# Reciprocal roots of a hybrid diffusion block: VectorE's Newton rounds or GpSimd's power

## The chip, the cores and the metric

The kernel runs on one core of a Trainium2 chip. The metric is the device time of one execution in microseconds. A core has five engines that run side by side, each with its own queue in a fixed order: TensorE (PE, matmuls and transposes), VectorE (DVE), ScalarE (ACT), GpSimd (POOL) and SyncE (SP, which only issues DMAs here). PE's weight loads are listed as PEld.

## The reference

Two layers of a diffusion backbone on 512 latent tokens and 256 context tokens of width 1024, in float32. Each layer is a mixer of four parallel branches (grouped-query attention with rotary positions, Mamba-2 SSD in both directions, S5, a gated short convolution), merged by gates and projected, then an expert-choice mixture of 16 SwiGLU experts. The context tokens leave after the first layer's experts. A reciprocal root of a mean of squares stands in five places:

```python
def rmsnorm(x, g):
    y = xf * lax.rsqrt(jnp.mean(xf * xf, axis=-1, keepdims=True) + RMS_EPS)
    return (y * g.astype(F32)).astype(x.dtype)
h_l = modulate(rmsnorm(x, norm_mix_g[i]), mod_l[0], mod_l[1])           # before the mixer
ql = axial_rope(rmsnorm(heads(q_l, ATTN_HEADS), q_norm_g), ...)         # q and k heads, width 64
return rmsnorm(y * jax.nn.silu(z), norm_g)                              # SSD, width 512
expert_choice_ffn(modulate(rmsnorm(x, norm_ffn_g[i]), ...), ...)        # before the router
return rmsnorm(x, final_norm_g)                                         # at the end
```

## The kernel before, in words

Tokens stand in tiles of 128 on the partitions: tiles 0 and 1 are context, 2 to 5 latent. `run` calls, for each layer, `mixer` (norm, branches, merge) and `moe`. Weights are streamed from HBM by SyncE; dense products split each operand into a high and a low part and take three matmuls (L99 to L101, the splits are L114 on ScalarE and L115 on VectorE).

`rsqrt` (L118) computes out = (x*scale + eps)^-0.5 for n numbers per partition. L124 forms v, L125 and L126 make a first guess by a shift and a subtraction on the bits, and three Newton rounds follow: L134 to L136 in the long form, three instructions a round, or L130 and L131 in the short one, two a round after a scaling of v in L128. All of it is on VectorE, 12 instructions long or 10 short. It is called 30 times:

- `norm` (L337), once a layer, n=6: the root of all six tiles, then the scaling of each tile (L339), then transposes (L344) and modulation (L347 to L349). It is marked high priority.
- `finish` in `ssd` (L846), once per tile (6 and 4), n=1: squares summed by ScalarE (L844), the root, y times root and gain (L847), transposes (L850). GpSimd does S L819 (half of the heads), y L835 (first layer) and segr L800 here.
- `attention` (L919), three times a layer, n=12 for keys and n=24 for two halves of the queries: sums of squares (L907), the root, R times root (L922), copies on GpSimd (L928), transposes (L929).
- `merge` (L574), once per tile (6 and 4), n=1, the short form: the root scales the router's logits (L580) and the rows that the experts gather (L594). Output projections (L99 to L101) of the next tile run beside it. After the last latent tile `places` (L1514 to L1518) takes the top tokens per expert on VectorE, and `gather` makes indices (L1536) and fetches rows with indirect DMAs from GpSimd's queue (L1538). Weight loads from a certain one on wait until the first gather has started (`wafter`).
- `last` in `moe` (L1681), twice at the very end, n=2: the final norm of two tiles each (L1680 sums, L1684 to L1686 scale, L1687 stores).

While a branch works through its chain, matmuls of gates, short convolution and modulation weights ("filling", psmm tiles) are laid into TensorE's queue beside it. The order in each engine's queue is not the program's: a list scheduler fixes it when the program is built, by priority and by its own model of how long each instruction takes. Semaphores for the dependences are added after that.

Of the kernel before, what the change touches and what calls it, by code (L numbers as in the profile page):

```python
# [9 lines left out]
F32 = mybir.dt.float32  # L10
# [3 lines left out]
I32 = mybir.dt.int32  # L14
AF = mybir.ActivationFunctionType
OP = mybir.AluOpType
# [42 lines left out]
class Kern:  # L59
# [58 lines left out]
    def rsqrt(self, pool, out, x, scale, eps, n, short=False):  # L118

        nc = self.nc  # L120
        v = pool.tile([128, n], F32, name="rs_v", tag=f"rsv{n}")
        y = pool.tile([128, n], F32, name="rs_y", tag=f"rsy{n}")
        t = pool.tile([128, n], F32, name="rs_t", tag=f"rst{n}")
        nc.vector.tensor_scalar(v, x, scale, eps, op0=OP.mult, op1=OP.add)  # L124
        nc.vector.tensor_scalar(t.bitcast(I32), v.bitcast(I32), 1, None, op0=OP.logical_shift_right)  # L125
        nc.vector.tensor_scalar(y.bitcast(I32), t.bitcast(I32), -1.0, float(0x5F3759DF), op0=OP.mult, op1=OP.add)  # L126
        if short:
            nc.vector.tensor_scalar(v, v, -0.5, None, op0=OP.mult)  # L128
            for i in range(3):
                nc.vector.tensor_scalar(t, y, y, v, op0=OP.mult, op1=OP.mult)  # L130
                nc.vector.tensor_scalar(out if i == 2 else y, t, 1.5, y, op0=OP.add, op1=OP.mult)  # L131
            return
        for i in range(3):
            nc.vector.tensor_mul(t, y, y)  # L134
            nc.vector.scalar_tensor_tensor(t, t, -0.5, v, op0=OP.mult, op1=OP.mult)
            nc.vector.scalar_tensor_tensor(out if i == 2 else y, t, 1.5, y, op0=OP.add, op1=OP.mult)  # L136

    def constants(self, pool, first, last):

# [6 lines left out]
    def setup(self):  # L146
        nc, tc, I = self.nc, self.tc, self.I
        self.cp = cp = self.ctx.enter_context(tc.tile_pool(name="cp", bufs=1))
        self.vt = "a"
        self.filling = True  # L150
        cT = cp.tile([128, 8, 2], F32, name="cT")
        nc.sync.dma_start(cT, I["cT"])
        self.cst = {}
        self.constants(cp, "ident", "one")
        self.ident = self.cst["ident"]
        self.identb = cp.tile([128, 128], BF16, name="identb")
        nc.vector.tensor_copy(self.identb, self.ident)
        th = cp.tile([128, 8, 2], F32, name="cth")
        nc.scalar.activation(th, cT, AF.Tanh, scale=0.5)
        self.cpad = cp.tile([128, 8, 32], F32, name="cpad")  # L160
        nc.vector.memset(self.cpad, 0.0)
        nc.vector.tensor_scalar(th, th, 1.0, 0.5, op0=OP.add, op1=OP.mult)
        nc.vector.tensor_mul(self.cpad[:, :, 0:2], th, cT)
        self.gm = cp.tile([128, 2, 2, 8], F32, name="gm")
        nc.scalar.dma_start(self.gm, I["gm"])
        self.bmT = cp.tile([128, 2, 48], F32, name="bmT")
        nc.scalar.dma_start(self.bmT, I["bmT"])
        self.modT, self.amod = {}, {}
        self.affT = cp.tile([16, 768], F32, name="affT")
        dr = lambda nm, *s: tc.dram_tile(list(s), F32, name=nm)  # L170

        self.xs = dr("xs", 512, D)
        self.xc = dr("xc", 256, D)
        self.mrow = {(l, q): dr(f"mrow{l}{q}", 2, D) for l in range(2) for q in (2, 5)}
        self.zs = dr("zs", 768, 512)
        self.ys = [dr(f"ys{b}", 128, 4, 768) for b in range(4)]
        self.gs = [dr(f"gs{b}", 8, 128, 768) for b in range(4)]

        self.s5w = dr("s5w", 6, 128, self.S5W)
        self.s5r = dr("s5r", 128, 24)  # L180

        self.hr = [[dr(f"hr{l}{s}", n, D) for s, n in enumerate((512, 256)[:2 - l])] for l in range(2)]
        self.afd = [[dr(f"afd{l}{s}", n, 16) for s, n in enumerate((512, 256)[:2 - l])] for l in range(2)]
# [1709 lines left out]
```

## Time and profile before

| what | value |
|---|---|
| median of 3 runs | 3041.78 us (3039.12 to 3045.5) |
| the profiled execution, its own time | 3042.23 us |
| its span, first to last instruction | 3040.5 us |
| mean granted TensorE clock | 0.971 of full speed |
| busy: PE, DVE, ACT, POOL | 2771.3, 1561.6, 786.6, 518.7 us |
| HBM traffic | 222 GB/s over the span |

A line of the timeline gives the start, the length, the engine, the line of the kernel, the operation, the tile written and the tile read with their shapes, and in brackets how long the engine had stood idle before and what released it. Several like instructions in a row are merged (x3). In the waits, a line says who waited for whom, us in total, how often, and the longest.

### The profile page before, as it was taken

The page shows a single profiled execution, that of the slowest core. Times are in us where ns is not written, and L with a number is a line of the kernel's source. Part 1 is how long each engine was busy: PE and PEld are TensorE (multiplying, and loading weights), DVE is VectorE, ACT ScalarE, POOL GpSimd, SP SyncE. Part 2 cuts the span into 40 slices and gives each one's busy share as a digit, 9 for nine tenths or more (in the row PEclk, how much of TensorE's full clock was granted, in tenths as well). Part 3 has the DMA queues.
Part 4 walks back from the last instruction along what each step waited for, and adds up shares of the span by engine and source line. Part 5 has one row for each costly group of instructions (what it writes and reads, how often), then busy time and mean ns, then how long its engine had stood idle before and what let it go on. Part 6 is the DMA issues. An engine that isn't in the chain of part 4 may idle for free. (4 is left out here: it accounts for less than half of the span.)

```text
span 3040.5 us, 47083 instructions
## 1 busy us (share of the span) xinstructions
PE 2771.3 (91%) x18626; PEld 1817.4 (60%) x18626; DVE 1561.6 (51%) x3583; ACT 786.6 (26%) x1749; POOL 518.7 (17%) x693
## 2 busy tenths in 40 slices
PE   7999978999999979899999989999999996998887
PEld 4866756787878964344333358577877883332223
DVE  5468588555516664544431354768564454322223
ACT  4354223325622310001110133323364221000001
POOL 1022075120004122111111010400200221100001
PEclk9999989999999989999999989999999997999999
DMA  7324523411146559899999843264214577999997
GB/s 240 108 72 124 164 86 113 132 38 59 56 155 218 184 191 384 337 392 345 361 374 399 337 150 106 61 213 166 80 50 158 168 272 291 409 409 409 409 409 299
DMA packets 332542, 678.69 MB, mean 223 GB/s; under 512 B 22945, under 2 KB 198305, under 8 KB 331554
## 3 DMA queue, kind: packets, MB, share of 16 engines
q1 hardware_dynamic: 297712, 610.31, 55.5%
q10 hardware_dynamic: 27666, 43.19, 3.9%
q0 software_dynamic: 6944, 22.19, 2.4%
q8 instruction: 147, 2.41, 0.3%
q14 instruction: 73, 0.60, 0.1%
HBM read 613.09 MB, written 60.94 MB: 222 GB/s over the span
## 5 line engine op out<-in xcount | busy, mean ns | idle before, releaser
L1578 PE MATMUL psa<-we,X 128*64 128x512 f32 (+1 forms) x4096 | 583.9, 491 | 37.0 <-DMA we<-in_w_exp_gate_dram 18.7
L1578 PEld LDWEIGHTS psa<-we,X 128*64 128x64 f32 (+1 forms) x4096 | 203.5, 123 | 391.6 <-issue 273.1
L99 PE MATMUL psmm<-hH,fwH 128*128 128x512 f32 x984 | 371.4, 377 | 7.7 <-DVE xpad L640 3.8
L101 PE MATMUL psmm<-hH,fwL 128*128 128x512 f32 x984 | 365.9, 372 | 2.2 <-DVE fwL L115 2.2
L100 PE MATMUL psmm<-hL,fwH 128*128 128x512 f32 x984 | 365.8, 372 | 0.0
L1610 PE MATMUL psa<-we,hidT 128*64 128x512 f32 x992 | 234.4, 610 | 18.6 <-ACT hidT L1598 13.0
L99 PEld LDWEIGHTS psmm<-hH,fwH 128*128 128x128 f32 x984 | 189.5, 193 | 50.3 <-issue 12.9
L101 PEld LDWEIGHTS psmm<-hH,fwL 128*128 128x128 f32 x984 | 189.4, 192 | 31.8 <-issue 5.2
L100 PEld LDWEIGHTS psmm<-hL,fwH 128*128 128x128 f32 x984 | 189.9, 193 | 30.8 <-issue 8.4
L1591 ACT ACTIVATE hid<-psa 128x512 f32<-128x512 f32 (+1 forms) x48 | 25.2, 526 | 547.7 <-PE psa L1578 481.3
L1610 PEld LDWEIGHTS psa<-we,hidT 128*64 128x64 f32 x992 | 68.7, 139 | 159.9 <-issue 115.7
L115 DVE TENSOR_TENSOR fwL<-fr,fwH 128x1024 fp32r<-128x1024 f32 (+1 forms) x100 | 109.0, 1091 | 101.1 <-ACT fwH L114 91.8
L1592 DVE SCALAR_TENSOR_TENSOR hid<-hid,psa 128x512 f32<-128x512 f32 (+1 forms) x48 | 28.7, 598 | 254.0 <-ACT hid L1591 254.0
L1618 DVE SCALAR_TENSOR_TENSOR y<-psa,ag,m 64x512 f32<-64x512 f32 x62 | 46.5, 750 | 204.6 <-PE psa L1610 204.0
L475 POOL TENSOR_TENSOR merged<-merged,tgm 128x512 f32<-128x512 f32 (+1 forms) x48 | 62.6, 1324 | 479.1 <-DVE tgm L473 478.8
L1565 POOL TENSOR_TENSOR X<-X,modT 128x512 f32<-128x512 f32 x40 | 42.9, 1083 | 521.8 <-DVE X L1564 452.8
L99 PE MATMUL psa<-cwH,hH 128*128 128x256 f32 (+1 forms) x432 | 123.3, 285 | 1.3 <-DVE R L909 1.2
L101 PE MATMUL psa<-cwH,hL 128*128 128x256 f32 (+1 forms) x432 | 122.2, 283 | 0.0
L100 PE MATMUL psa<-cwL,hH 128*128 128x256 f32 (+1 forms) x432 | 122.1, 283 | 0.0
L114 ACT CAST fwH<-fr 128x1024 fp32r<-128x1024 f32 (+1 forms) x100 | 89.5, 896 | 123.4 <-DMA fr<-in_w_in_dram 67.3
L420 ACT ACTIVATE tg<-psmm 128x512 f32<-128x512 f32 x96 | 50.7, 529 | 191.4 <-PE psmm L101 188.0
L1593 DVE TENSOR_TENSOR hid<-hid,psa 128x512 f32<-128x512 f32 (+1 forms) x48 | 28.7, 598 | 135.0 <-PE psa L1578 134.4
(566 smaller groups left out, 5714.4 us busy)
## 6 DMA issues: line engine op xcount, KB each, us to landing
we<-in_w_exp_gate_dram SPq DMA_DIRECT2D x128, 1024.0 KB
we<-in_w_exp_up_dram SPq DMA_DIRECT2D x128, 1024.0 KB
we<-in_w_exp_down_dram SPq DMA_DIRECT2D x128, 1024.0 KB
fr<-in_w_mod_dram SPq DMA_DIRECT2D x96, 512.0 KB
fr<-in_w_in_dram SPq DMA_DIRECT2D x64, 512.0 KB
raw<-in_w_in_dram SPq DMA_DIRECT2D x36, 512.0 KB
gs<-tg ACTq DMA_DIRECT2D x32, 384.0 KB
tgm<-gs SPq DMA_DIRECT2D x32, 384.0 KB
```

What stands on the lines that cost most here:

```text
L99: self.nc.tensor.matmul(ps, ah, bh, start=start and i == 0, stop=False)
L100: self.nc.tensor.matmul(ps, ah, bl, start=False, stop=False)
L101: self.nc.tensor.matmul(ps, al, bh, start=False, stop=stop and i == n - 1)
L114: self.nc.scalar.copy(h, x)
L115: self.nc.vector.tensor_sub(l, x, h.bitcast(F32))
L420: nc.scalar.activation(tg[:, o:o + n], self.cm(w, m, o, n), AF.Tanh, scale=0.5)
L475: (V if i == 3 else nc.gpsimd).tensor_add(dst, dst, t)
L1565: nc.gpsimd.tensor_add(X[:, hk], X[:, hk], Bm[:, 24 + h * 4:28 + h * 4, s:s + 1].to_broadcast([128, 4, 128]))
L1578: self.lastup = nc.tensor.matmul(ps[s][j * c:(j + 1) * c], X[s][:, k, r:r + c], w(k)[:, j * n:(j + 1) * n], start=k == 0, stop=k == 7, ski ...
L1592: V.scalar_tensor_tensor(hid, hid, 1.0, g, op0=OP.add, op1=OP.mult)
L1610: ins = nc.tensor.matmul(ps[j * c:(j + 1) * c], lh, w(k)[:, j * n:(j + 1) * n], start=k == 0, stop=k == 7, skip_group_check=True)
L1618: self.lasty = V.scalar_tensor_tensor(Y[s][r, nn], ps[j * c:(j + 1) * c], got[s][1][r, e:e + 1], m5[s][r, nn], op0=OP.mult, op1=OP.mult)
```

## The change

`rsqrt` becomes two instructions on GpSimd: v = x*scale + eps, and v to the power -0.5, the exponent read from a tile `half` that VectorE fills once at the start. Both forms, long and short, become this one; the tiles for the guess and the rounds go. No call site is edited.

```diff
         v = pool.tile([128, n], F32, name="rs_v", tag=f"rsv{n}")
-        y = pool.tile([128, n], F32, name="rs_y", tag=f"rsy{n}")
-        t = pool.tile([128, n], F32, name="rs_t", tag=f"rst{n}")
-        nc.vector.tensor_scalar(v, x, scale, eps, op0=OP.mult, op1=OP.add)
-        nc.vector.tensor_scalar(t.bitcast(I32), v.bitcast(I32), 1, None, op0=OP.logical_shift_right)
-        nc.vector.tensor_scalar(y.bitcast(I32), t.bitcast(I32), -1.0, float(0x5F3759DF), op0=OP.mult, op1=OP.add)
-        if short:
-            nc.vector.tensor_scalar(v, v, -0.5, None, op0=OP.mult)
-            for i in range(3):
-                nc.vector.tensor_scalar(t, y, y, v, op0=OP.mult, op1=OP.mult)
-                nc.vector.tensor_scalar(out if i == 2 else y, t, 1.5, y, op0=OP.add, op1=OP.mult)
-            return
-        for i in range(3):
-            nc.vector.tensor_mul(t, y, y)
-            nc.vector.scalar_tensor_tensor(t, t, -0.5, v, op0=OP.mult, op1=OP.mult)
-            nc.vector.scalar_tensor_tensor(out if i == 2 else y, t, 1.5, y, op0=OP.add, op1=OP.mult)
+        nc.gpsimd.tensor_scalar(v, x, scale, eps, op0=OP.mult, op1=OP.add)
+        nc.gpsimd.tensor_tensor(out, v, self.half[:, :n] if n == 1 else self.half.to_broadcast([128, n]), op=OP.pow)
...
         self.cp = cp = self.ctx.enter_context(tc.tile_pool(name="cp", bufs=1))
+        self.half = cp.tile([128, 1], F32, name="half")
+        nc.vector.memset(self.half, -0.5)
```

## Rows read from the trace of the kernel before

**Rows 1.** Page, part 1: busy us (share of the span) and instructions.
```profile
PE 2771.3 (91%) x18626; PEld 1817.4 (60%) x18626; DVE 1561.6 (51%) x3583; ACT 786.6 (26%) x1749; POOL 518.7 (17%) x693
```

**Rows 2.** Groups by line, VectorE: busy us, mean ns, idle before.
```profile
L134 DVE TENSOR_TENSOR rs_t<-rs_y 128x1 f32<-128x1 f32 (+4 forms) x60 | 14.9, 249 | 1.4
```

**Rows 3.** Timeline, VectorE: first and last step of three roots, SSD and attention.
```profile
313.28 0.15 DVE L124 TENSOR_SCALAR rs_v<-ssy 128x1 f32<-128x1 f32 x1 [0.84 <-ACT z L844]
...
315.39 0.16 DVE L136 SCALAR_TENSOR_TENSOR rsy<-rs_t,rs_y 128x1 f32<-128x1 f32 x1
255.71 0.15 DVE L124 TENSOR_SCALAR rs_v<-ssy 128x1 f32<-128x1 f32 x1
...
264.05 0.16 DVE L136 SCALAR_TENSOR_TENSOR rsy<-rs_t,rs_y 128x1 f32<-128x1 f32 x1
641.11 0.17 DVE L124 TENSOR_SCALAR rs_v<-ssq 128x24 f32<-128x24 f32 x1
...
646.20 0.18 DVE L136 SCALAR_TENSOR_TENSOR rq<-rs_t,rs_y 128x24 f32<-128x24 f32 x1
```

**Rows 4.** PE's waits: 200 to 330 (two), 600 to 700, 2140 to 2210, 1935 to 1995.
```profile
PE psa L850 <- DVE y L847: 6.7, 5, 2.5
PE psmm L99 <- DVE xpad L640: 1.0, 1, 1.0
PE psa L929 <- POOL kd L928: 3.8, 4, 1.6
PE psa L929 <- POOL kd L928: 2.2, 3, 1.5
PE psmm L99 <- DVE cv L643: 1.1, 1, 1.1
```

**Rows 5.** Groups by line and shape, GpSimd: busy us, mean ns, idle before.
```profile
L819 POOL TENSOR_TENSOR S<-S,E 128x128 f32<-128x128 f32 x40 | 21.8, 546 | 83.4 <-DVE S L818 80.0 <-PE psmm L101 1.2 <-DVE rs_y L126 1.1
L1538 POOL DMA_INDIRECT xg<-hr,xi x20 | 20.0, 1002 | 79.3 <-DVE xi L1536 39.0 <-DVE x L1017 23.3 <-issue 6.4
L603 POOL MEMSET xpad<- 128x1 f32 x72 | 3.9, 124 | 156.8 <-DVE cv L619 100.2 <-PE psb L1610 24.6 <-DVE modT L208 24.5
```

**Rows 6.** Timeline, GpSimd and VectorE: single instructions at 262, 676 and 1941.
```profile
262.31 0.46 POOL L819 TENSOR_TENSOR S<-S,E 128x128 f32<-128x128 f32 x1 [0.42 <-DVE S L818]
...
676.54 0.73 POOL L917 TENSOR_TENSOR R<-R,tp 128x256 f32<-128x256 f32 x1 [2.10 <-DVE rs_v L124]
676.58 0.73 DVE L125 TENSOR_SCALAR rs_t<-rs_v 128x24 int32<-128x24 int32 x1
...
1941.53 1.04 POOL L800 TENSOR_TENSOR segr<-cst,dt 128x512 f32<-128x512 f32 x1 [0.27 <-PE psa L806]
```

**Rows 7.** Timeline, VectorE: the roots of the two layers' first norms.
```profile
14.05 0.17 DVE L124 TENSOR_SCALAR rs_v<-ss 128x6 f32<-128x6 f32 x1 [9.49 <-ACT junk L335]
...
16.27 0.17 DVE L136 SCALAR_TENSOR_TENSOR rstd<-rs_t,rs_y 128x6 f32<-128x6 f32 x1
...
1752.89 0.17 DVE L124 TENSOR_SCALAR rs_v<-ss 128x6 f32<-128x6 f32 x1 [1.23 <-ACT junk L335]
...
1758.15 2.08 DVE L339 TENSOR_SCALAR x<-x,rstd 128x1024 f32<-128x1024 f32 x3
```

**Rows 8.** Timeline, VectorE: last root and indices of layer 0's router; layer 1's last logits.
```profile
1114.86 0.12 DVE L124 TENSOR_SCALAR rs_v<-ss 128x1 f32<-128x1 f32 x1
...
1122.83 0.15 DVE L1536 CAST xi<-fi 128x1 int32<-128x1 f32 x1
...
2529.06 0.23 DVE L580 SCALAR_TENSOR_TENSOR lg<-psa,rstd,cb 128x16 f32<-128x16 f32 x1 [0.29 <-PE psa L578]
```

**Rows 9.** Windows: us, busy (instructions) of PE, PEld, DVE, ACT, POOL; PEclk, DMA, GB/s.
```profile
2705.00:3016.00 311.00, 260.06 (x1168) 86.20 (x1165) 73.54 (x114) 19.48 (x33) 14.67 (x15) 1.00 1.03 406
```

**Rows 10.** Timeline, VectorE: the final norm's first sum, and its last four scalings.
```profile
3028.76 0.15 DVE L1680 TENSOR_TENSOR ss<-ss 128x2 f32<-128x2 f32 x1
...
3034.36 0.48 DVE L1685 SCALAR_TENSOR_TENSOR x<-x,rs,g 128x256 f32<-128x256 f32 x1
...
3035.42 0.35 DVE L1686 TENSOR_SCALAR x<-x,rs 128x256 f32<-128x256 f32 x1
```

## The prediction, made before the changed kernel ran

> **What bounds the kernel now.** I read the page's busy times first: TensorE is busy 91% of the span, VectorE 51%, GpSimd 17% [rows 1]. A change that moves work from VectorE to GpSimd can therefore gain only where TensorE, or the weight stream, stands still because of a reciprocal root. So I looked next at the roots themselves (the groups by line), then at when each of the 30 calls starts and ends (the timeline), and last at what TensorE waits for in those stretches (the waits).
>
> The roots take 340 VectorE instructions: 20 calls of 12 and 10 short ones of 10. The largest group, L134 with 60 of them, takes 14.9 us [rows 2]; with the other groups of L124 to L136 in that view it is about 69 us, 2.3% of the span. Nearly all of it lies beside TensorE work. Undisturbed, a chain of 12 takes 2.3 us (313.28 to 315.55); where the scheduler has laid other VectorE work between its steps it takes 8.5 us (255.71 to 264.21) or 5.3 us (641.11 to 646.38) [rows 3]. That is what TensorE notices: it waited 6.7 us for L847 (the line behind the root) in the first layer's SSD, and 3.8 and 2.2 us for the copies that follow the root in the two attentions [rows 4].
>
> **The change, part by part.** Each call becomes two GpSimd instructions: a multiply-add T, and a power X of n elements per partition. Added in all: 60 GpSimd instructions, and one VectorE memset at the start, before VectorE has anything to do, so at nothing.
>
> *Price of T.* The nearest rows are a 128x1 memset, 0.124 us, and a two-input 128x128 multiply, 0.546 us [rows 5]. I take 0.2, nearer the first, as it reads one tensor of few elements.
>
> *Price of X.* No power runs in the trace. From below, the memset, 0.12 us. From above I charge every element per partition as much as that whole 128x128 multiply, on top of the 1.0 us of GpSimd's slowest small instruction, the indirect DMA (1002 ns): 1.0 + 0.46n, with 0.46 for an undisturbed multiply [rows 5, 6]. That is 1.5 us for n=1 and 12 us for n=24. I take X = 0.65 + 0.06n as an estimate: a fixed part between multiply and indirect DMA, and 40 times the multiply's step per element, since the multiply grows from 0.46 us at 128 elements to 1.04 us at 512, 1.5 ns each [rows 6]. So 0.7 us for n=1 or 2, 1.0 for 6, 1.4 for 12, 2.1 for 24. With three handovers between engines at 0.1 us each (an estimate; a step of an undisturbed chain starts 0.2 us after the one before and takes 0.15) the root of one element is ready 1.2 us after its sum instead of 2.3 or more, and that of 24 after 2.6 instead of 4.1, the mean of the four such calls, of which 641.11 is the longest [rows 3].
>
> Now place by place, in order of time. Each term is what TensorE, or the end, gets back.
>
> - First norm (n=6): the chain runs from 14.05 to 16.44 with VectorE otherwise idle [rows 7]. After: 0.3 + 0.2 + 1.0 = 1.5 us instead of 2.4. Scaling and transposes follow at once: 0.8.
> - SSD, first layer, six calls: waits of 6.7 us for L847 and 1.0 us for L640, which stands in VectorE's queue among the steps of a root [rows 4]. The longest, 2.5 us, follows an undisturbed chain and can shrink by 2.3 - 1.2 = 1.1 us; the other 5.2 us could go altogether, 6.3 at best. What is late next is L847 itself, in order behind chunk work on VectorE. I take half: 3.0.
> - Attention, both layers, six calls (four of 24, two of 12): with roots 1.5 us (n=24) and 2.4 us (n=12) earlier, up to 5 of the 6.0 us of waiting [rows 4] could go; gate matmuls fill TensorE up to that point and hide the rest. Half: 2.5.
> - Router of layer 0: the last context tile's root (1114.86 to 1120.40) is interleaved with the top-k of the latent tokens on a full VectorE, and the gather's indices (1122.83) come behind both [rows 8]. Adding up the spacing of its ten starts gives 1.65 us. The first expert matmul waits for that gather: 1.5. The other nine router roots lie beside output-projection matmuls: 0.
> - Second norm: 1752.89 to 1758.11, 5.2 us, because a weight split (L115, 1.21 us) and small work run between the steps; scaling starts at 1758.15 [rows 7]. After, the root is ready at 1754.4, and scaling can start behind L115 at 1755.25. Of these 2.9 us some goes to matmuls that wait for w_mod: 1.6.
> - SSD, second layer: a wait of 1.1 us for L643 [rows 4] and another of 1.0 for L640, which follow root steps in VectorE's queue: 0.8.
> - Router of layer 1, last tile: the logits (L580) start at 2529.06, released by TensorE, so the root isn't late there [rows 8]; but its steps delay the copies of hT that TensorE needs: 0.8. The weight stream runs at a DMA share of 1.03 from 2705 to 3016 [rows 9], and at 1.02 from 2557 on, so later gains inside that expert stage are worth nothing; this one counts, since the stream restarts behind the gather.
> - Final norm, two calls of n=2: on VectorE they run one behind the other, and the last scaling ends at 3035.77 [rows 10]. After: the first root is ready at 3028.91 + 0.3 + 0.2 + 0.7 = 3030.1, the second at 3031.0. VectorE needs 1.41 us for the four scalings behind a root (3034.36 to 3035.77), so the eight run from 3030.1 to 3032.9: 2.9, of which I take 2.2, since ScalarE's scalings run beside them and may end later.
>
> Sum: 0.8 + 3.0 + 2.5 + 1.5 + 1.6 + 0.8 + 0.8 + 2.2 = 13.2 us. The profiled execution took 3042.2 us (span 3040.5), so 3029.0; the median of the runs is 0.4 us below the profiled one, which I leave aside.
>
> **A rule weighed.** GpSimd and VectorE hold each other up already: a step of the root on 24 elements, whose like took 0.17 us [rows 3], took 0.73 us and ended with the GpSimd addition that had begun 0.04 us earlier [rows 6]. The Trainium skill (SBUF — State Buffer, Who interferes with whom) says that the two share one pair of ports, that whoever issues first holds it for the whole instruction, and that the other is blocked, not throttled. The trace agrees, 0.73 against 0.17 us. By that rule each power could stop VectorE for its whole length, which is rival B.
>
> **Rivals.**
> - A, the slow side: the power is dear per element. Place: the six attention roots, whose R (L922) and kd copies (L928) wait for them. At 0.65 + n*p against today's 4.1 us (n=24, four times) and 4.3 us (n=12, twice), attention loses 120p - 18 us, counted with 0.5 us for T and handovers. That eats the 10.7 us of the other places from p = 0.24 us (6.4 us for n=24) on. At p = 0.46 attention loses 37 us; if gate matmuls cover a third it is 25, the other places keep 10, and the time is 3057. For: nothing in the trace bounds it. Against: GpSimd's rows grow by only 1.5 ns per element [rows 6].
> - B, gain given back: the powers (about 30 us in all, 36 with T) block VectorE, and GpSimd's queue, in order, holds S L819 and y L835 behind a root that waits for its sum. SSD and attention then gain nothing and ten SSD calls cost 0.3 us each: 13.2 - 6.3 + 3 leaves 3.9, 3038.3. For: the 0.73 us above. Against: 69 us of VectorE work goes, twice what comes to GpSimd.
> - C, the scheduler: it fixes every queue's order from its own durations, so 340 instructions fewer and 60 more give another order in all stages. SSD and attention pack roots, chunk work and filler into the same queues, and an order that leaves TensorE 15 us more idle there eats the gain: 3044. This can also help. For: chains of 2.3 us stretched to 8.5 show how freely it interleaves.
> - That the change doesn't do what it says: the root may fail to come off VectorE only if the power were lowered to other instructions, which I give no chance of its own.
>
> **How the numbers follow.** Forecast (a quick power, 3020 to 3036): 0.50. A: 0.22. B: 0.18. C: 0.10. With X at the memset's price all places give at most 22 us: 3020. With X at its upper end 3057 to 3069. I leave out a tenth at either end: 3019 to 3055; the forecast's own range is 3020 to 3036. This kernel's runs tell about 0.2%, 6 us, from no change. Faster than that: the forecast and a little of B and C, 0.52; within: most of B, half of C, a little of A, 0.24; slower: most of A and some of C, 0.24.
>
> **What would show it.** In the changed profile: groups L124 to L136 gone from VectorE and its busy time some 65 us lower; a GpSimd power group whose mean for n=1 is near 0.7 us and for n=24 near 2 us (A: over 6); TensorE's wait for L847 in the first SSD down from 6.7 to about 3 us; scaling in the second norm 2 to 3 us after its sums; the last scaling within 6 us of the last sum of squares. Wrong are: a power over 2 us for one element; TensorE's waits for S L819 or kd L928 grown (B); or a gain or loss in a stage that holds no root (C).

## The result, and the profile after

The changed kernel takes 3070.3 us, median of 4 runs (3069.01 to 3071.5), beside 3043.5 us for the kernel before on the same chip: ratio 1.0089, 95% interval 1.0072 to 1.0105. That is some 27 us slower, where 13 us faster was forecast; it lies above the widest range stated (3019 to 3055) and above the slow end of rival A (3069). In the code after, lines behind `rsqrt` are 11 lower than before; T is L122 and the power L123.

Part 1 of the page, against [rows 1]:

```profile
PE 2776.5 (90%) x18626; PEld 1825.5 (59%) x18626; DVE 1502.9 (49%) x3244; ACT 788.8 (26%) x1749; POOL 565.9 (18%) x753
```

VectorE lost 59 us of busy time and GpSimd gained 47. TensorE executes the same 18626 matmuls; it is 5 us longer busy with them and stands idle 22 us longer (291.7 us of the span instead of 269.2).

The powers themselves, groups by line and shape on GpSimd (busy us, mean ns, idle before):

```profile
L123 POOL TENSOR_TENSOR rq<-rs_v,half 128x24 f32<-128x24 f32 x4 | 16.7, 4170 | 0.3
L123 POOL TENSOR_TENSOR rstd<-rs_v,half 128x1 f32<-128x1 f32 x10 | 5.6, 562 | 0.8
L123 POOL TENSOR_TENSOR rsy<-rs_v,half 128x1 f32<-128x1 f32 x10 | 5.5, 551 | 0.8
L123 POOL TENSOR_TENSOR rq<-rs_v,half 128x12 f32<-128x12 f32 x2 | 4.6, 2290 | 0.2
L123 POOL TENSOR_TENSOR rstd<-rs_v,half 128x6 f32<-128x6 f32 x2 | 2.7, 1346 | 0.2
L123 POOL TENSOR_TENSOR rs<-rs_v,half 128x2 f32<-128x2 f32 x2 | 1.5, 755 | 0.2
```

A line through these is 0.40 us + 0.157 us per element: a quick root for one number (0.56 us), as long as the whole Newton chain for 24 (4.17 us).

TensorE's waits after, in the stretches of [rows 4]: first layer's SSD (200 to 330), the two attentions (590 to 700, 2140 to 2215):

```profile
PE psa L839 <- DVE y L836: 2.8, 2, 1.9
...
PE psa L918 <- POOL kd L917: 9.2, 3, 4.7
...
PE psa L918 <- POOL kd L917: 9.1, 3, 4.5
```

The SSD wait fell from 6.7 to 2.8 us; those in the attentions rose from 3.8 and 2.2 to over 9. One attention call of layer 1, from the timeline of all engines:

```profile
2170.25 0.41 DVE L896 TENSOR_REDUCE ssq<-sq 128x4 f32<-128x256 f32 x1
...
2170.75 0.21 POOL L122 TENSOR_SCALAR rs_v<-ssq 128x24 f32<-128x24 f32 x1 [2.76 <-DVE ssq L896]
...
2171.04 4.17 POOL L123 TENSOR_TENSOR rq<-rs_v,half 128x24 f32<-128x24 f32 x1
...
2173.49 0.40 PE L100 MATMUL psmm<-hL,fwH 128*128 128x512 f32 x1
2175.19 0.72 POOL L906 TENSOR_TENSOR R<-R,tp 128x256 f32<-128x256 f32 x1
2175.94 1.22 DVE L911 TENSOR_TENSOR R<-R,rq 128x1024 f32<-128x1024 f32 x1 [4.40 <-POOL R L906]
2177.30 1.65 POOL L917 COPY kd<-R 128x128 f32<-128x128 f32 x6 [1.39 <-DVE R L911]
2177.64 0.94 PE L918 MATMUL psa<-cst,kd 128*128 128x128 f32 x3 [3.75 <-POOL kd L917]
2178.24 0.78 PE L101 MATMUL psmm<-hH,fwL 128*128 128x512 f32 x1
```

Read it downwards: the power ends at 2175.21; the addition to R (L906), whose result L911 reads, stands behind it in GpSimd's queue and costs another 0.72 us; TensorE's last filling matmul ends at 2173.89, 3.75 us before the transposes can start; and the filling matmul behind that idle time takes 0.78 us instead of 0.40: the granted clock has gone from 2.4 to 1.2 GHz.

The same call in the kernel before:

```profile
2168.50 0.42 DVE L907 TENSOR_REDUCE ssq<-sq 128x4 f32<-128x256 f32 x1
...
2174.78 0.18 DVE L136 SCALAR_TENSOR_TENSOR rq<-rs_t,rs_y 128x24 f32<-128x24 f32 x1
...
2175.93 0.40 PE L100 MATMUL psmm<-hL,fwH 128*128 128x512 f32 x1
...
2176.77 0.80 PE L929 MATMUL psa<-cst,kd 128*128 128x128 f32 x3 [0.43 <-POOL kd L928]
```

From the last sum of squares to the transposes that wait for it, the chain of the four calls with 24 columns takes 7.7 us on average in both kernels. What became shorter is the filling work beside it: past that sum it lasted 5.5 to 7.5 us before, and lasts 3.2 to 3.7 us now. In layer 1 these were 30 and 25 filling matmuls, and now are 13 and 13.

Over whole attention windows the clock shows as PEclk (columns as in [rows 9]). First the changed kernel, 590 to 700 and 2140 to 2215; then the second window before (the first had 730 matmuls, also at 1.00):

```profile
590.00:700.00 110.00, 100.76 (x708) 85.81 (x705) 54.74 (x166) 37.84 (x96) 34.70 (x75) 0.94 0.24 75
2140.00:2215.00 75.00, 64.08 (x388) 55.56 (x388) 36.61 (x107) 20.93 (x40) 32.12 (x62) 0.93 0.17 50
```

```profile
2140.00:2215.00 75.00, 72.85 (x442) 61.96 (x440) 46.20 (x136) 26.27 (x52) 20.28 (x56) 1.00 0.21 64
```

Such a window is cut by the clock on the wall, so its count mixes what was laid there with how fast it ran. Counted from event to event, layer 1 shows what was laid (matmuls on TensorE):

| stretch of layer 1 | before | after |
|---|---|---|
| first transpose of the norm to last transpose of the SSD | 1217 | 1174 |
| from there to the attention's first transpose (L929) | 1034 | 998 |
| the attention, to its last transpose of that line | 321 | 302 |
| from there to the first expert matmul | 1952 | 2060 |

So 108 matmuls more come behind the attention, and only 19 of them left the attention itself; the stretches of SSD and S5 lost more. The last stretch takes 377 us instead of 351, and the first expert matmul of layer 1 comes at 2586.0 instead of 2556.5.

### The profile page after: what moved, and what is told of

It reads as the page before. It is cut to its first block, busy times and chain, and to the rows that moved or that the text cites. A ratio compares the mean times of both kernels' runs of the same rounds, so it can differ in the third digit from the quotient of the medians.

```text
span 3068.2 us, 46800 instructions
## 1 busy us (share of the span) xinstructions
PE 2776.5 (90%) x18626; PEld 1825.5 (59%) x18626; DVE 1502.9 (49%) x3244; ACT 788.8 (26%) x1749; POOL 565.9 (18%) x753
## 5 line engine op out<-in xcount | busy, mean ns | idle before, releaser
L99 PE MATMUL psmm<-hH,fwH 128*128 128x512 f32 x984 | 370.9, 377 | 13.4 <-DVE modT L196 5.2
L99 PEld LDWEIGHTS psmm<-hH,fwH 128*128 128x128 f32 x984 | 189.8, 193 | 54.5 <-issue 11.8
L99 PE MATMUL psa<-cwH,hH 128*128 128x256 f32 (+1 forms) x432 | 122.6, 284 | 0.6 <-DVE dtv L694 0.5
```

What stands on the lines that cost most here:

```text
L99: self.nc.tensor.matmul(ps, ah, bh, start=start and i == 0, stop=False)
```

## The experiments

Theory M: the scheduler counts the power as short and lays less filling work beside the root; on the chip the chain behind it ends later than the filling work, TensorE idles, drops to the low clock and does the rest of the filling later. Theory C: any new order costs this, whatever the roots last. All runs were timed over 5 rounds beside the kernel before; "+n us" below is what the ratio makes of 3043 us. In all variants a root is a power only at the sites named. Where they differ from the changed kernel in the constant -0.5, it stands in a column of an old tile. The edits are shown shortened. Places in an order are compared in the traces, by operation, shapes and tile names without buffer numbers.

**e1: the same order, no long power.**

```diff
-        nc.gpsimd.tensor_tensor(out, v, half, op=OP.pow)
+        nc.gpsimd.tensor_tensor(out, v, half, op=OP.mult if site == "attn" else OP.pow)
```

> The changed kernel, instruction for instruction in the same order on every engine, but in the six attention calls GpSimd multiplies by -0.5 where it took the power (so q and k are scaled wrongly there). Theory M (the long power of 12 and 24 columns starves TensorE, which idles, drops to the low clock and does the filling matmuls late): the instruction falls from 4.17 us to under 0.4 us, TensorE's waits on kd in the two attention windows from 9 us each to under 3 us, the granted clock there comes back to near 1.00, and 15 to 25 us of the 27 are gone: 3045 to 3055 us. Theory C (the new order alone costs the time, whatever the power lasts): the waits elsewhere stay and the time stays at 3064 to 3070 us.

Measured: 3049.9 us, ratio 1.0025 (1.0014 to 1.0035). The groups on GpSimd, the waits in the two attentions, and the window 2140 to 2215 of this run:

```profile
L127 POOL TENSOR_TENSOR rq<-rs_v,half 128x24 f32<-128x24 f32 x4 | 0.9, 227 | 0.3
L127 POOL TENSOR_TENSOR rq<-rs_v,half 128x12 f32<-128x12 f32 x2 | 0.4, 208 | 0.2
```

```profile
PE psa L939 <- POOL kd L938: 1.5, 2, 1.3
...
PE psa L939 <- POOL kd L938: 1.9, 3, 1.0
```

```profile
2140.00:2215.00 75.00, 73.01 (x470) 61.09 (x469) 42.80 (x109) 30.17 (x70) 19.87 (x56) 1.00 0.18 57
```

TensorE's order is that of the changed kernel in all but 2 of 18626 places, and 20 of the 27 us are gone. That the order came out the same, though only the operation differs, says that the scheduler counts a power no longer than a product, which takes 0.23 us on the chip where the power takes 4.17. The six powers together are 4 x (4.17 - 0.23) + 2 x (2.29 - 0.21) = 19.9 us longer than the six products: in this order every microsecond of them is paid in full. Some 7 us are left that are not the length of these six. In the profiles they are the rest of a gain and a larger loss: the first transpose of the second norm comes at 1755.0 instead of 1760.3, but from there to the first expert matmul of layer 1 it takes 811 us instead of 796.

**e2 to e4, e12: which sites cost.** Only the tuple of sites that take the power changes.

```diff
-POW = ('norm', 'ssd', 'attn', 'router', 'final')
+POW = ('norm', 'ssd', 'router', 'final')      # e2
+POW = ('attn',)                               # e3
+POW = ('norm', 'router', 'final')             # e4
+POW = ('ssd',)                                # e12
```

> The changed kernel with the attention's six roots back on VectorE by Newton rounds; all other roots are powers. Theory M: the loss sat in the attention, so 20 to 40 us of it go and the time is at or under that of the kernel before, 3030 to 3044 us; first expert matmul of layer 1 back at about 2555 us. Theory C (any change of the scheduler's input gives a bad order): slower than the kernel before by 10 us or more, 3055 to 3070 us.

> The kernel before with the attention's six roots alone as powers. Theory M: most of the loss is there with these six instructions alone, 3055 to 3075 us, with waits on kd of 7 us or more in each attention window. Theory C: the loss is spread over the stages and belongs to the order of the whole, so this is as likely 3040 as 3060 us, and the stages without attention carry it.

> The kernel before with the roots of the two norms, the router and the final norm as powers, those of the SSD layer and the attention by Newton rounds. By the terms that the changed kernel bore out (second norm about 4 us, final about 2 us, first norm about 1 us) 3034 to 3039 us. If the order of the scheduler decides whatever the roots cost, the gain does not add up: 3044 us or more.

> The kernel before with the roots of the SSD layers alone as powers. By the wait on the SSD output that fell from 6.7 to 2.8 us in the changed kernel: 3 to 4 us faster, 3039 to 3041 us. If the wait only moves (the S5 stage behind it, which has no root, had 7 to 8 us more idle TensorE time in each layer of the changed kernel): 3044 to 3052 us, with that idle time in the S5 stage of layer 1.

| run | us | ratio (95%) | |
|---|---|---|---|
| e2, all but attention | 3054.4 | 1.0045 (1.0027 to 1.0062) | +14 us |
| e3, attention alone | 3058.7 | 1.0058 (1.0042 to 1.0075) | +18 us |
| e4, norms, router, final | 3048.6 | 1.0020 (1.0008 to 1.0032) | +6 us |
| e12, SSD alone | 3052.3 | 1.0032 (1.0019 to 1.0045) | +10 us |

The plain medians, against 3044.2 us for the kernel before (3043.1 for e12), give 10, 15, 4 and 9 us. The three parts (e3, e4 and e12) add up to 34 us, not 27, so they overlap. e3 agrees with M. e2, e4 and e12 do not: these roots hold no power of 12 or 24 elements, and they lose time as well. So either the order costs by itself (C), or M holds for the short powers too. e12's expectation looked for the loss in the S5 stage of layer 1; from 1990 to 2150 TensorE idles only 2 us more than before.

**e5: one instruction more,** meant to give another order and nothing else. One early memset of a column on VectorE, all roots as before. The trace shows that the order hardly changed: TensorE's is that of before in all but 2 of 18626 places.

> The kernel before with one more instruction: an early memset of one column on VectorE, in which no engine's work depends; all roots stay Newton rounds. Itself it is worth under 0.2 us. If only what the roots cost counts: 3042 to 3046 us, as before. If any new input gives the scheduler another order and the order of the kernel before is one of the better ones: 3047 to 3055 us, and that much of the loss in the other runs is the order and not the power.

Measured: 3042.7 us, ratio 1.0003 (0.9994 to 1.0011). That is the time of the kernel before with the order of before, so it says nothing on C. What bears on C are e7 and e16 below: their orders on TensorE differ from that of before in 950 and 6042 places, and neither is slower. Another order costs nothing as such.

**e6, e7: the attention of layer 1 alone,** as powers and, in the same order on every engine, as products; TensorE's order is that of the kernel before up to there.

```diff
+POW = ('attn1',)          # the power in layer 1's three calls; e7: op=OP.mult there
```

> The kernel before with the three roots of the attention of layer 1 alone as powers, the constant written by GpSimd just ahead of them; TensorE's order is that of the kernel before up to this attention. Theory M (the root is counted short and lasts long: less filling work is laid beside it, TensorE idles, then runs at the low clock): nothing changes up to 2150 us; waits on kd of 7 us or more in this window, granted clock there about 0.91, the first expert matmul of layer 1 10 to 16 us later, 3054 to 3060 us. Theory C (order alone): a wait on kd as before, 2 to 3 us, and the rest as the order falls.

> The same program as that with the powers in the attention of layer 1 alone, the same order on every engine, with a product by -0.5 in place of these three powers (q and k of layer 1 are scaled wrongly). Theory M: the wait on kd falls to under 2 us, the granted clock there to 1.00, and 8 to 12 us of the loss are gone: 3044 to 3049 us. Theory C: time as with the powers.

Measured: e6 3051.2 us, ratio 1.0025 (1.0015 to 1.0035), 8.3 us of waiting for kd in this attention; e7 3043.1 us, 1.0001 (0.9992 to 1.0010). TensorE's order is the same in both, with 12 and 13 filling matmuls behind the last sum of squares in the two calls of 24 columns. The 8 us are the length of the powers, which are together 10 us longer than the products. And the other half: a root of 0.45 us in place of 4 us gains nothing against the kernel before. The filling work had hidden the long root, so there was nothing to win there.

**e8, e9: the power, with the Newton rounds counted beside it.** The dead Newton chain runs on VectorE and the multiplication by the root is put behind it. In e8 its first instruction wrote the buffer that the power reads, so the two ran one after the other; e9 has a buffer of its own. The order on TensorE is the same in both.

```diff
+                if l == 1:
+                    last = self.rsqrt(rp, rd, ss, 1.0 / 64, EPS, NT * nh, own=True)   # e9; nobody reads rd
...
-                V.tensor_mul(Rv, Rv, rq)
+                mul = V.tensor_mul(Rv, Rv, rq)
+                tc.add_manual_dep(mul, last, NoSync)      # order on VectorE only
```

> The powers in the attention of layer 1 alone, and beside each the Newton rounds on VectorE as before, into a tile that nobody reads; the multiplication by the root is put behind them on VectorE. The chip waits for the power, the scheduler counts the long Newton chain too. If the scheduler's short count of the root is what leaves TensorE without filling work: the filling matmuls are laid as before, the wait on kd is at most 4 us and the time 3042 to 3048 us. If the length of the power on the chip alone decides, wherever the filling work is laid: kd waits of 7 us and 3053 us or more.

> Mends the run with power and Newton rounds in the attention of layer 1: there the first Newton instruction wrote the buffer that the power reads and so waited for it. Now it has a buffer of its own, so that power and Newton rounds run beside each other; the order of the instructions is the same on every engine. If the scheduler's short count of the root is what leaves TensorE without filling work: wait on kd in this attention at most 4 us, granted clock 1.00, 3042 to 3048 us. If the length of the power decides even where the filling work was laid for Newton rounds: kd waits of 7 us or more, 3050 us or more.

Measured: e8 3056.5 us, ratio 1.0046 (1.0033 to 1.0059); e9 3045.0 us, 1.0006 (0.9997 to 1.0016). e8 didn't test what it was meant to; its expectation of a time near the kernel before failed because the chain on the chip had become power plus Newton, 9 us. Beside e9 it shows again that what counts is how long the chain is on the chip against what was laid for it. The waits and the window 2140 to 2215 of e6, then of e9:

```profile
PE psa L940 <- POOL kd L939: 8.3, 2, 4.7
```

```profile
2140.00:2215.00 75.00, 66.56 (x408) 58.06 (x406) 38.27 (x99) 24.77 (x51) 30.64 (x61) 0.95 0.17 50
```

```profile
PE psa L946 <- POOL kd L945: 2.7, 2, 1.9
```

```profile
2140.00:2215.00 75.00, 72.29 (x432) 61.96 (x430) 44.88 (x135) 25.54 (x49) 31.15 (x60) 0.98 0.20 64
```

The same three powers on the chip (one of the two with 24 columns takes 4.17 us as in e6, the other 5.11), and the wait falls from 8.3 to 2.7 us, because more filling matmuls stand ahead of the transposes: 29 and 24 behind the last sum of squares, where e6 has 12 and 13. In the timeline of e9 one such call reads:

```profile
2168.19 1.21 DVE L118 TENSOR_TENSOR fwL<-fr,fwH 128x1024 fp32r<-128x1024 f32 x1
...
2168.32 5.11 POOL L130 TENSOR_TENSOR rq<-rs_v,cth 128x24 f32<-128x24 f32 x1
...
2173.08 0.18 DVE L144 TENSOR_TENSOR rs_t<-rs_y 128x24 f32<-128x24 f32 x1
...
2173.30 0.18 DVE L145 SCALAR_TENSOR_TENSOR rs_t<-rs_t,rs_v 128x24 f32<-128x24 f32 x1
2173.41 0.74 POOL L929 TENSOR_TENSOR R<-R,tp 128x256 f32<-128x256 f32 x1
2173.51 0.67 DVE L146 SCALAR_TENSOR_TENSOR rd<-rs_t,rs_y 128x24 f32<-128x24 f32 x1
...
2174.72 0.39 PE L102 MATMUL psmm<-hH,fwH 128*128 128x512 f32 x1
2175.88 0.80 PE L946 MATMUL psa<-cst,kd 128*128 128x128 f32 x3 [0.77 <-POOL kd L945]
```

Filling matmuls run to 2175.11 and TensorE idles 0.77 us, where it idled 3.75 us in the changed kernel behind a power that was almost 1 us shorter.

**e10, e11: the sites that looked best,** final norm alone, and with it the second norm.

> The kernel before with the two roots of the final norm alone as powers, the constant written by GpSimd; the order on TensorE and ScalarE is that of the kernel before. These roots stand at the end of the chain of waits with nothing beside them: 1.5 to 2.2 us faster, 3041 to 3042.5 us, at the edge of what can be told from no change. If the shorter root is hidden even here: no difference in the last 10 us of the trace.

> The kernel before with the roots of the second norm and of the final norm as powers; up to the end of layer 0 TensorE's order is that of the kernel before. If the gain seen at the second norm (3 to 4 us from the last expert matmul to the norm's first transpose) is kept, it is 3037 to 3040 us, faster than both kernels. If it is given back behind it, because the order that follows lays less filling work beside the SSD layer: the stretch from that transpose to the first expert matmul of layer 1 is 5 us or more longer than 796 us, and 3043 to 3049 us.

Measured: e10 3041.7 us, ratio 0.9997 (0.9988 to 1.0006), the expected time, which can't be told from no change; e11 3048.5 us, 1.0015 (1.0004 to 1.0026). The 3 to 4 us at the second norm are given back: from its first transpose to the first expert matmul of layer 1 it is 806 us (1756.3 to 2562.7) instead of 796. A single profile's stretches vary between executions of one order or nearly one (796 to 799 us here in the kernel before, e5, e10 and e13), so this number alone would hardly carry it; the median does.

**e13, e14: the same for the short powers.** The SSD powers of e12 with Newton rounds beside them; then all powers of the changed kernel, with Newton rounds beside those of norms, SSD and attention.

> The roots of the SSD layers alone as powers, and beside each the Newton rounds on VectorE into buffers that nobody reads, with the multiplication by the root behind them on VectorE. If the scheduler's short count of the root cost the 9.8 us of the run with SSD powers alone: 3042 to 3046 us, and the granted clock between 1925 and 1990 us back near 1.00. If the power in GpSimd's queue costs them: 3050 us or more.

> All roots as powers, as in the changed kernel, and beside those of the norms, the SSD layers and the attention the Newton rounds on VectorE as in the run before, with the consumer behind both. If the scheduler's count is the whole cause: 3042 to 3048 us, 22 us or more of the 27 gone, though GpSimd does the same 20 us of powers more. If the long powers and GpSimd's queue carry a part whatever the order: 3050 to 3062 us.

Measured: e13 3042.3 us, ratio 1.0000 (0.9990 to 1.0010), against +10 us in e12; e14 3040.0 us, 0.9993 (0.9983 to 1.0004), against +27 us. All of the loss is gone, with the same powers in GpSimd's queue. The counts of layer 1, from event to event, are 1181, 1022, 321 and 2000 in e12; in e13 and e14 they are 1217, 1034, 321 and 1952, as in the kernel before. So the order made for the short count of these roots costs the 10 us. Whether the length of the powers counts in that order, as it does in the attention, is open: no run has e12's order with a product. The window 1925 to 1990 (SSD of layer 1) of e12 and of e13; before, it held 293 matmuls at 1.00:

```profile
1925.00:1990.00 65.00, 60.36 (x247) 38.18 (x247) 42.48 (x108) 20.25 (x49) 20.62 (x35) 0.87 0.22 61
```

```profile
1925.00:1990.00 65.00, 60.54 (x292) 38.41 (x292) 51.47 (x160) 22.55 (x55) 21.11 (x37) 1.00 0.32 90
```

TensorE is busy for as long, but with 45 matmuls fewer at a lower clock. The timeline of e12 shows one way in which that came about:

```profile
1943.34 1.53 DVE L857 SCALAR_TENSOR_TENSOR y<-y,rsy,par 128x512 f32<-128x512 f32 x1 [2.75 <-ACT E L817]
...
1944.79 0.34 DVE L828 SCALAR_TENSOR_TENSOR S<-Gge,dt,S 128x128 f32<-128x128 f32 x1
...
1945.20 0.45 POOL L829 TENSOR_TENSOR S<-S,E 128x128 f32<-128x128 f32 x1 [0.89 <-DVE S L828]
...
1945.71 0.43 PE L830 MATMUL psa<-x_tok,S 128*128 128x64 f32 x2 [1.15 <-POOL S L829]
```

The scheduler has put the scaling by the early root (L857) ahead of S (L828) in VectorE's queue; before, it came behind (1948.26, S at 1942.90). TensorE waits 1.15 us for S instead of 0.49, and from 1946.7 to 1957.0 its granted clock is half. From 1945 to 1955 it ran 25 matmuls at a granted clock of 0.59, where the kernel before ran 53 at 1.00.

**e15, e16: is a short root worth anything once the filling work is laid?** e15 is e14 with the attention's roots by Newton rounds alone. e16 replaces the Newton rounds beside the norm and SSD powers by copies on ScalarE.

```diff
-                self.last = self.rsqrt(pool, None, x, scale, eps, n)         # e15: Newton rounds, result unread
+                d = pool.tile([128, n], F32, name="rs_d", tag=f"rsv{n}")     # e16
+                self.last = nc.scalar.copy(d, x)
+                for i in range(7):
+                    self.last = nc.scalar.copy(d, d)
```

> As the run before (all roots as powers, Newton rounds beside those of the norms and the SSD layers), but the attention's six roots by Newton rounds alone. If a shorter root is worth its time once the filling work is laid: final norm 1.5 us, router 1 to 2 us, and no long powers in the attention, 3036 to 3040 us, faster than both kernels. If it is worth nothing: 3040 to 3045 us.

> As that, but beside the powers of the norms and the SSD layers stand eight copies on ScalarE in place of the Newton rounds, ahead of the consumer in the scheduler's order only; on the chip the consumer waits for the power. If the scheduler counts the copies and the short root is worth its time: 3033 to 3039 us. If the copies hold up ScalarE's own work or aren't counted: 3044 to 3055 us.

Measured: e15 3037.2 us, ratio 0.9974 (0.9965 to 0.9983), 8 us faster than the kernel before; e16 3036.4 us, 0.9967 (0.9954 to 0.9979), 10 us faster. Both beat both kernels, e16 with an order that differs from that of before in 6042 places. e16 is not told from e15 by these intervals. Where in the kernel the 8 to 10 us are won was not followed up.

## Why the prediction was wrong, step by step

- **The step that failed** is in the attention term: "gate matmuls fill TensorE up to that point and hide the rest". The cover was taken over from the trace of before. It is not a property of the stage; it is what the scheduler lays for the root that it counts. With the roots shorter in its account the filling work lasted 3.2 to 3.7 us past the last sum of squares instead of 5.5 to 7.5, and the power, as long as the Newton rounds before, came out uncovered. The term was +2.5; e1 puts the powers' length in this order at -20, and e3 puts the attention alone at -18. The other terms share the step: each took its gain under the order of before, and the orders made for the short roots cost 10 us for the SSD alone (e12) and 6 us for norms, router and final norm (e4).
- **The price of X** was mis-sized per element: 0.65 + 0.06n against 0.40 + 0.157n; near for n=1 (0.7 against 0.56), half of the true value for n=24 (2.1 against 4.17). By rival A's own formula this would have been harmless: 120 x 0.157 - 18 is 0.8 us of loss, under its break-even of 0.24 per element. So A, as put, is not what happened either: its sum, too, set the power against today's chain under today's cover.
- **What is queued behind the wait** was named only for SSD. In the attention the addition to R stands behind the power and adds 0.72 us in a call of 24 columns. It was not tried apart.
- **SSD, first layer, 3.0:** the wait named did shrink as forecast (6.7 to 2.8 us; 2.4 in e12), and yet SSD powers alone cost 10 us (e12). In e13 the wait is back at 6.3 us and the time is that of the kernel before. So this wait was no measure of a gain.
- **SSD, second layer, 0.8:** the two waits named, 1.1 and 1.0 us, became 2.8 (L632) and 0.6 us (L629). No gain.
- **Second norm, 1.6:** from the first step of the root to the scaling it took 5.26 us [rows 7]; after it is 1.69 (1758.85 to 1760.54). More than forecast in its place; e11 shows it given back in the 800 us behind.
- **First norm, 0.8:** 1.65 us from T to the scaling, where 1.5 was forecast, and the first transpose comes 0.9 us earlier (17.95 instead of 18.85). But the granted clock is full from 31.1 us on instead of 23.7, and the first product of the normed tokens (L99) starts at 39.71 instead of 36.74. In e1, e2 and e4, with the same power, it starts at 38.1 or later, in every run with Newton rounds alone there at 37.7 or earlier: 1 to 3 us were lost.
- **Router of layer 0, 1.5:** its last root took 0.8 us (1118.92 to 1119.74), but the gather's indices came 9.4 us behind it (1129.15) instead of 2.4 [rows 8]. No gain. The 1.65 us that the prediction gives for its ten steps before does not come out of the trace: their lengths alone add up to 1.87.
- **Router of layer 1, 0.8:** from the last logits to the first expert matmul it is 27.5 us (2558.49 to 2586.0), before 27.4. No gain there.
- **Final norm, 2.2:** from the first sum to the start of the last scaling 4.15 us (3057.91 to 3062.06) against 6.66 [rows 10]: 2.5. Right. It stands at the end, with no filling work to lose.
- **The rivals.** C came nearest, with a tenth of the chance and 15 us where it needed over 20. It is not that any other order costs (e7, e16); the cause is an order made for a shorter root. The sign named for B, a grown wait for kd, did come, but not from a block: with products in the same places of GpSimd's queue the wait is 1.5 and 1.9 us (e1), and in e9 Newton steps of 0.18 us begin and end on VectorE inside a power of 5.11 us. What holds VectorE up there is the 128x256 addition: the step at 2173.51 takes 0.67 us and ends with it, as in [rows 6]. By these rows a power in progress does not stop VectorE. The other sign, a grown wait for S in the first SSD, is small: 1.5 us instead of 1.1.

What stays open: the scheduler's own figure for a power isn't seen in any trace. That it is short is concluded from e1 and e7, where a product in its place leaves the order as it is, and from e9, e13 and e14, where counting a longer chain beside the same powers took the loss away. For the short powers it is open how much of their loss is length and how much the order itself.

## What to carry to other kernels

Before you shorten a step that is hidden by laid work, ask who laid that work and from which length: a scheduler that counts the step shorter gives less cover, and then the true length is paid in full. Where a latency is hidden there is nothing to win by shortening it (e7), and a new instruction whose real length the scheduler doesn't know is best given a stand-in of the right length in its account (e14 to e16). To tell length from order, replace the instruction by a cheaper one of the same form: where the order stays, as it did here, the difference is the length alone.

## What the runs showed of the hardware that was not expected

- A power on GpSimd costs 0.157 us per element and partition beyond 0.40 us, while a product of the same shape takes 0.23 us for 24 elements and 0.21 for 12.
- Of the powers of 24 elements, one in e8, e9 and e14 each takes 5.11 or 5.12 us and all others 4.17 or 4.18. In e9 the long one begins 0.13 us after a split on VectorE of 1.21 us (2168.19). In the other call of e9 a like split and Newton steps begin inside the power, and neither they nor the power are longer:

```profile
2192.88 4.17 POOL L130 TENSOR_TENSOR rq<-rs_v,cth 128x24 f32<-128x24 f32 x1
...
2195.20 0.18 DVE L144 TENSOR_TENSOR rs_t<-rs_y 128x24 f32<-128x24 f32 x1
...
2195.55 1.23 DVE L118 TENSOR_TENSOR fwL<-fr,fwH 128x1024 fp32r<-128x1024 f32 x1
```

- A short wait can cost more through TensorE's clock than it lasts: in e12 an idle time of 1.15 us was followed by some 10 us at half clock, where the kernel before idled 0.49 us and kept the full clock. From 1945 to 1955 TensorE, 93% busy, finished 25 matmuls instead of 53.
